# Another written order for the entry of layer 0

## The chip, the cores and the metric

The kernel runs on one core of one Trainium2 chip. The core has TensorE for matrix products (PE in the profile, its weight loads PEld), VectorE (DVE), ScalarE (ACT), GpSimd (POOL) and SyncE (SP, which here only issues loads). Products are written to PSUM, everything else lies in SBUF. The metric is the time of one execution on the device in microseconds (us), as the median of several.

## The reference

Two layers of a transformer over 512 tokens `x` and 256 context tokens `ctx`, width 1024, all in float32. Only the start of layer 0 matters here:

```python
mod = silu_c @ ada_w[l] + ada_b[l]            # for x; modc the same from c_ctx, for ctx
sh1, sc1, g1, sh2, sc2, g2 = split(mod, 6)    # parts 0 to 5
a  = rmsnorm(h, norm1_g[l]) * (1 + sc1) + sh1
ac = rmsnorm(hc, norm1_g[l]) * (1 + csc1) + csh1
u, v, q, k, vv = split(a @ w_in, ...)
kc, vvc = split(ac @ w_in[:, KV_START:], ...)
```

So before the first large product (here `q` and `k`) a small product has to give the shift and scale columns (`ada`), and each token's root mean square has to be known.

## The kernel before

Tokens lie along the free dimension, the width in eight tiles of 128 partitions (`k` = 0 to 7): `hx[k]` is 128x512 of `x`, `hc[k]` 128x256 of `ctx`. Every float32 operand of a large product is split into two fp32r parts, a rounded one by ScalarE (`copy`) and the difference by VectorE or POOL. `mm3` (lines 115 to 117) makes three products out of them, high by high, high by low, low by high. Weights `raws[k]` are split by `w_split(k)`, the difference at line 456 on POOL. All this is in the function `even`.

The order of work in the entry is written out by hand. `run` (line 48) puts each instruction behind the one that was written before it on its engine: `chain` for TensorE, `act`, `dve`, and "SP" for the loads. All these show as L49. What isn't written with them is placed by a planner, which simulates the times of the whole program.

The steps that are touched:

- `ada_step(ps, k, slab)`: one k of the product of the silu of both conditions (`cst`, 32 columns) with a slab of `ada_w`, in four column groups; TensorE. Eight of them make half a part (512 columns). `half_load(j, h)` loads the slabs of half h of part j, in two tiles of 1 MB (tag `ar`, 4 buffers). Parts: 1 scale, 0 shift.
- `half_row(ps)`: ScalarE copies the result from PSUM to `row`, TensorE turns it into columns in a bank `pt`. `half_mod(j, h, v, who)`: VectorE adds the bias and, for the scale, computes (m + 1) * gain into `self.mod`; `who` is 0 for `x`, 1 for `ctx`.
- `sums(acc, T)`: TensorE sums the squares, VectorE takes the inverse root (lines 144 to 148) and makes diagonals of it (line 185). `spread(rd)`: TensorE spreads a diagonal to a row `rx` (for `x`) or `rc` (for `ctx`) in a bank. There are three banks of tag `b`.
- `scale(k)`: VectorE multiplies `hx[k]` by the scale column and `rx`; ScalarE takes the high part. `low(k)`: VectorE takes the low one. `lagged` runs the two so that `low` is one k late. `ctx_square`, `ctx_scale`, `ctx_low`: the same for `ctx`, into `CP`.
- `project(k)`: 12 products of 512 columns into four PSUM halves `accx` (q and k for `x`). The shift is not in `scale`: `shift_cols(h)` puts the shift columns behind the ctx columns of `CP` (256 + 2), the ctx products `accc` carry them along, and they are added later as `bc`. `shifted(k)` then makes the operand with shift for the later `v0` products.
- `warm(t, n)`: n products whose result nobody reads.
- `ada_some`, `ada_ahead`: steps and loads of parts 2 to 5, which go on during the v0 products.

Of the kernel before, what the change touches and what calls it, by code (L numbers as in the profile page):

```python
# [6 lines left out]
F32 = mybir.dt.float32  # L7
# [4 lines left out]
ALU = mybir.AluOpType  # L12
AX = mybir.AxisListType.X

P = 128
D = 1024
KT = D // P
# [10 lines left out]
class Builder:  # L28
# [17 lines left out]
    def run(self, key, fn, *args, **kw):  # L46

        with self.tc.issue_after(self.tail[key].ins) if key in self.tail else ExitStack():
            self.tail[key] = fn(*args, **kw)  # L49
        return self.tail[key]  # L50
# [269 lines left out]
    def even(self):  # L320
        tc, nc, a = self.tc, self.nc, self.a
# [15 lines left out]
        for k in range(0, KT, 2):  # L337
            t = self.load(Rh, a["xT"][k * P:(k + 2) * P, :].rearrange("(k p) t -> p k t", p=P), [P, 2, TX], f"hx{k}")
# [18 lines left out]
        def half_load(j, h):  # L357

            out = []
            for k in (0, 4):  # L360
                t = self.adap.tile([P, 4, 512], F32, name=self.uid("ar"), tag="ar", bufs=4)
                c = j * D + h * 512
                src = a["ada0"][k * P:(k + 4) * P, c:c + 512].rearrange("(k p) c -> p k c", p=P)
                self.last_slab = run("SP", nc.sync.dma_start, t, src)
                out += [t[:, i, :] for i in range(4)]
            return out

        def chain(fn, *args, **kw):
            return run("PE", fn, *args, **kw) if head else fn(*args, **kw)  # L369

        def ada_step(ps, k, t):

            w = t.shape[-1] // 4
            for q in range(4):
                chain(nc.tensor.matmul, ps[32 * q:32 * q + 32, :w], cst[:, k, :], t[:, w * q:w * q + w], start=k == 0,
                      stop=k == KT - 1, skip_group_check=True)
# [18 lines left out]
        def half_row(ps):  # L395

            row = self.tmp("t")[:, :P]
            act(nc.scalar.copy, row, ps[:, :P])
            pt = self.bank()[:, :P]
            chain(nc.tensor.transpose, pt, row, self.ident)  # L400
            return row, pt.rearrange("p (q w) -> p q w", q=4)

        def half_mod(j, h, v, who):

            c = slice(j * KT + 4 * h, j * KT + 4 * h + 4)
            m = self.mod[who][:, c]
            dve(nc.vector.tensor_tensor, m, v[:, :, who], self.adab[:, c], ALU.add)
            if j:
                dve(nc.vector.scalar_tensor_tensor, m, m, 1.0, self.gain(0, 0)[:, 4 * h:4 * h + 4], ALU.add, ALU.mult)

        idle = self.wide()

        def warm(t, n):

            for _ in range(n):
                chain(nc.tensor.matmul, idle[:, :P], self.ones, t, start=True, stop=True, skip_group_check=True)
# [12 lines left out]
        def ada_some():  # L429
            if loaded:  # L430
                j, k, t = loaded.pop(0)
                if k == 0:
                    ps_of[j] = self.fill()
                ada_step(ps_of[j], k, t)
                if k == KT - 1:
                    ada_out(j, 2, ps_of.pop(j), self.bank())

        raws = []
# [11 lines left out]

        W = {}

        def w_split(k):
            t = self.adap.tile([P, 2, 512], F32R, name=self.uid("wq"), tag="wq", bufs=2) if k in (2, 5) else self.slot()
            act(nc.scalar.copy, t[:, 0, :], raws[k])
            nc.gpsimd.tensor_tensor(t[:, 1, :], raws[k], t[:, 0, :].bitcast(F32), ALU.subtract)  # L456
            W[k] = [(t[:, 0, c:c + P], t[:, 1, c:c + P]) for c in range(0, 512, P)]

        self.tail, run, head = {}, self.run, [1]
# [1 line left out]
        def act(fn, *args, **kw):  # L461
            return run("ACT", fn, *args, **kw)

        def dve(fn, *args, **kw):
            return run("DVE", fn, *args, **kw)

        sq = self.squares(hx, TX)
        slabs = {(1, 0): half_load(1, 0)}
# [15 lines left out]
        def sums(acc, T):  # L484
            rd = self.rstd_diag([(acc, T)], 1.0 / D)[0]
            self.tail["PE"], self.tail["DVE"] = self.last_sum, self.last_diag
            return rd

        def spread(rd):
            rows = self.bank()[:, :rd.shape[-1]]  # L490
            chain(nc.tensor.matmul, rows, self.ones, rd, start=True, stop=True)
            return rows

        rd = sums(sq, TX)
        ps0 = self.fill()
        for k in range(KT):
            ada_step(ps0, k, slabs[1, 0][k])
            if k == 5:
                rx = spread(rd)
            warm(slabs[1, 0][k][:, :P], 2)  # L500
        row, pt = half_row(ps0)
        warm(row, 8)
        w2 = [self.wide(), self.wide()]
        accx = [w[:, h * 512:(h + 1) * 512] for w in w2 for h in range(2)]
        keys = (0, 1, 4, 5)
# [12 lines left out]
        def shift_cols(h):  # L518
            for who in range(2):
                m = self.mod[who][:, 4 * h:4 * h + 4]  # L520
                hi, lo = [CP[:, 4 * h:4 * h + 4, i, TC + who] for i in range(2)]
                act(nc.scalar.copy, hi, m)
                dve(nc.vector.tensor_tensor, lo, m, hi.bitcast(F32), ALU.subtract)

        def shifted(k):
            for h, A, who in ((hx[k], axx[k], 0), (hc[k], axc[k], 1)):
                sh = self.modcol(0, 0, k, who)
                act(nc.scalar.activation, A[0], h, AF.Identity, bias=sh)
                dve(nc.vector.scalar_tensor_tensor, A[1], h, sh, A[0].bitcast(F32), ALU.add, ALU.subtract)
# [3 lines left out]
        def ctx_square(i):  # L533
            t = self.tmp("tq"[i % 2])[:, :TC] if i else csq
            act(nc.scalar.activation, t, hc[i], AF.Square)
            if i:
                dve(nc.vector.tensor_tensor, csq, csq, t, ALU.add)
# [8 lines left out]
        def project(k):  # L546
            for n in range(4):
                chain(self.mm3, accx[n], W[k][n], axx[k], k == 0, k == KT - 1)

        def lagged(first, second, ks):  # L550
            ks = list(ks)
            for i, k in enumerate(ks):
                first(k)
                if i:
                    second(ks[i - 1])
            second(ks[-1])

        half_mod(1, 0, pt, 0)
        w_split(0)
        w_split(1)  # L560
        lagged(scale, low, range(4))
        half_mod(1, 0, pt, 1)
        w_split(2)
# [2 lines left out]
        project(1)  # L566
        for i in range(4):
            ctx_square(i)
        ps0 = self.fill()
        for i in range(KT):  # L570
            ada_step(ps0, i, slabs[1, 1][i])
        row, pt = half_row(ps0)
        half_mod(1, 1, pt, 0)
        lagged(scale, low, range(4, 8))
        half_mod(1, 1, pt, 1)
        w_split(4)
        for i in range(4, 8):
            ctx_square(i)
        for k in (2, 3, 4):
            project(k)  # L580
        with tc.issue_after(self.tail["PE"].ins), tc.issue_after(self.tail["DVE"].ins):
            rd = sums(csq, TC)
        for k in (5, 6, 7):
            w_split(k)
        for k in (5, 6):
            project(k)
        rc = spread(rd)
        ps0 = self.fill()
        for i in range(KT):
            ada_step(ps0, i, slabs[0, 0][i])  # L590
        lagged(ctx_scale, ctx_low, range(KT))
        row, pt = half_row(ps0)
        half_mod(0, 0, pt, 0)
        half_mod(0, 0, pt, 1)
        shift_cols(0)
        project(7)
        evens = [0.125 if key < 4 else 1.0 for key in keys]
        for n in range(4):
            act(nc.scalar.mul, qk[keys[n]][:, :TX], accx[n], evens[n])
        w2 = [self.wide(), self.wide()]  # L600
        accc = [w[:, h * 512:h * 512 + TC + 2] for w in w2 for h in range(2)]
        for k in range(KT):
            if k == 3:
                ps0 = self.fill()
                for i in range(KT):
                    ada_step(ps0, i, slabs[0, 1][i])
                row, pt = half_row(ps0)
                half_mod(0, 1, pt, 0)
                half_mod(0, 1, pt, 1)
                shift_cols(1)  # L610
            for n in range(4):
                run("PE", self.mm3, accc[n], W[k][n], (CP[:, k, 0, :], CP[:, k, 1, :]), k == 0, k == KT - 1)
            if k == 4:
                head.clear()
            if k == 5:
                for i in range(4):
                    shifted(i)
            if k > 4:
                ada_some()
                ada_ahead(1)  # L620
        for n in range(4):
            t = qk[keys[n]]
# [4 lines left out]
        for n in range(4):  # L627
            t = qk[keys[n]]
# [10 lines left out]
        for k in range(KT):  # L639
            W = self.unit(a["v0"][k * P:(k + 1) * P, :], 512)  # L640
            for tb in range(6):
                c = slice(tb * P, (tb + 1) * P)
# [4 lines left out]
        for ps in acc:  # L647
            h = Rv.tile([P, 512], F32R, name=f"vhi{len(vhi)}")
# [267 lines left out]
        for k in order:  # L916
# [7 lines left out]
            if k == 4:  # L924
                low = ins
# [1108 lines left out]
```

## Time and profile before

| | |
|---|---|
| median of 3 runs | 1567.02 us (1563.9 to 1568.08) |
| profiled execution | 1566.89 us |
| its span | 1565.1 us |
| TensorE busy | 1506.8 us, 96% |
| VectorE, POOL, ScalarE busy | 1079.9, 818.3, 734.4 us |
| granted TensorE clock, mean | 0.993 |

A row of the timeline gives start and duration in us, the engine, the line, the operation, the tile written and the tiles read, the shape, and how many equal ones were merged (x). In brackets stands the idle time of the engine before it and who ended it. A merged row covers the time from the first start to the last end, so that waits in between may lie in it. A row of the stages gives the window, then busy time and count of PE, PEld, DVE, ACT and POOL, then the granted clock, the busy share of the DMA engines and GB/s. A float32 product counts as two instructions.

### The profile page before, as it was taken

How to read it: one execution, taken by the hardware profiler on the slowest of the kernel's cores; microseconds unless marked ns; L12 is line 12 of the kernel's file. 1: busy time of each engine (PE TensorE's matmuls, PEld its weight loads, DVE VectorE, ACT ScalarE, POOL GpSimd, SP SyncE). 2: the span in 40 equal slices, each digit the busy share in tenths (PEclk: the TensorE clock that was granted, in tenths of full speed). 3: DMA queues.
4: the chain of work that ended last, by engine and by line, in shares of the span. 5: the costliest groups of instructions: out<-in, count | busy, mean ns of one | idle time of the engine just before them, and what ended most of it. 6: DMA issues, size and time to landing. Idle time of an engine off the chain costs nothing.

```text
span 1565.1 us, 25189 instructions
## 1 busy us (share of the span) xinstructions
PE 1506.8 (96%) x9647; PEld 1352.6 (86%) x9647; DVE 1079.9 (69%) x1920; ACT 734.4 (47%) x1515; POOL 818.3 (52%) x558
## 2 busy tenths in 40 slices
PE   6899999999999999999999999999999999999998
PEld 4667788889999999999999988777869889999997
DVE  5532788865688788888786487665657976666665
ACT  3434567563553333333333254555556544444444
POOL 1262231051256776677776454531314399888882
PEclk9999999999999999999999999999999999999999
DMA  9583100051223333454542212110224132323201
GB/s 334 188 315 128 45 21 1 8 194 68 68 83 117 115 113 112 142 168 137 167 169 68 80 59 63 56 35 15 66 104 162 55 120 90 114 89 115 89 21 54
DMA packets 55464, 162.27 MB, mean 104 GB/s; under 512 B 6192, under 2 KB 8624, under 8 KB 47664
## 3 DMA queue, kind: packets, MB, share of 16 engines
q1 hardware_dynamic: 48288, 135.37, 25.5%
q10 hardware_dynamic: 7056, 25.30, 5.0%
q8 instruction: 75, 1.23, 0.3%
q14 instruction: 45, 0.37, 0.1%
HBM read 158.55 MB, written 2.10 MB: 103 GB/s over the span
## 4 chain that ended last, share of the span: by engine, by line
PE 81%; DVE 10%; ACT 2%; issue 2%; POOL 0%; DMA 0%; DVEq 0%; ACTq 0%; POOLq 0%
PE pw L115 11%; PE pw L116 11%; PE pw L117 11%; PE pb L116 8%; PE pb L115 8%; PE pb L117 8%; PE pf L115 4%; PE pf L116 4%; PE pf L117 4%; PE pb L1844 2%; PE pb L1833 2%; PE pw L1795 1%; PE pw L1803 1%; PE pf L369 1%; DVE t L49 1%
## 5 line engine op out<-in xcount | busy, mean ns | idle before, releaser
L115 PE MATMUL pw<-ax,w 128*128 128x384 f32 (+2 forms) x716 | 227.4, 319 | 4.5 <-DVE q L49 1.9
L992 DVE SCALAR_TENSOR_TENSOR xT<-pb,mod,xT 128x512 f32<-128x512 f32 (+3 forms) x204 | 143.2, 708 | 127.7 <-PE pb L117 127.5
L116 PE MATMUL pw<-ax,w 128*128 128x384 f32 (+2 forms) x716 | 228.0, 319 | 2.4 <-DVE ax L49 2.4
L117 PE MATMUL pw<-ax,w 128*128 128x384 f32 (+2 forms) x716 | 227.6, 318 | 0.7 <-POOL w L456 0.6
L49 POOL TENSOR_TENSOR w<-raw,w 128x512 fp32r<-128x512 f32 x122 | 185.4, 1535 | 47.3 <-ACT w L49 47.2
L92 POOL TENSOR_TENSOR w<-raw,w 128x512 fp32r<-128x512 f32 (+1 forms) x70 | 103.4, 1483 | 168.7 <-ACT w L89 153.5
L49 POOL TENSOR_TENSOR w<-t,w 128x512 fp32r<-128x512 f32 x99 | 149.2, 1510 | 55.7 <-ACT w L49 55.7
L115 PE MATMUL pb<-hh,w 128*128 128x512 f32 x480 | 171.0, 356 | 1.2 <-DVE xT L992 1.2
L117 PE MATMUL pb<-hh,w 128*128 128x512 f32 x480 | 171.5, 357 | 0.4 <-DVE w L49 0.4
L116 PE MATMUL pb<-hh,w 128*128 128x512 f32 x480 | 171.1, 356 | 0.0
L115 PE MATMUL pw<-T,w 128*128 128x384 f32 (+1 forms) x508 | 157.3, 311 | 2.5 <-DVE hs L1200 1.2
L116 PE MATMUL pw<-T,w 128*128 128x384 f32 (+1 forms) x508 | 157.7, 311 | 1.2 <-DVE T L132 1.2
L117 PE MATMUL pw<-T,w 128*128 128x384 f32 (+1 forms) x508 | 157.7, 311 | 0.0
L115 PE MATMUL pf<-ax,w 128*128 128x256 f32 (+2 forms) x460 | 150.5, 327 | 2.8 <-DVE qf L264 1.0
L117 PE MATMUL pf<-ax,w 128*128 128x256 f32 (+2 forms) x460 | 149.3, 325 | 0.0
L116 PE MATMUL pf<-ax,w 128*128 128x256 f32 (+2 forms) x460 | 148.8, 324 | 0.0
L115 PEld LDWEIGHTS pw<-ax,w 128*128 128x128 f32 x716 | 136.1, 191 | 9.5 <-DVE q L49 2.6
L116 PEld LDWEIGHTS pw<-ax,w 128*128 128x128 f32 x716 | 136.7, 191 | 7.2 <-DVE ax L49 3.2
L117 PEld LDWEIGHTS pw<-ax,w 128*128 128x128 f32 x716 | 136.6, 191 | 3.7 <-POOL w L456 1.1
L49 POOL TENSOR_TENSOR hh<-hs,hh 128x768 fp32r<-128x768 f32 (+1 forms) x42 | 77.5, 1846 | 94.9 <-ACT hh L49 68.8
L49 POOL TENSOR_TENSOR w<-rawo,w 128x512 fp32r<-128x512 f32 x59 | 103.7, 1757 | 28.7 <-ACT w L49 28.7
L240 DVE SCALAR_TENSOR_TENSOR junk<-ar,cb 128x1024 bf16<-128x1024 f32 x64 | 105.6, 1650 | 0.0
(443 smaller groups left out, 3928.0 us busy)
## 6 DMA issues: line engine op xcount, KB each, us to landing
raw<-ffn_in SPq DMA_DIRECT2D x44, 1024.0 KB, 5.4
ar<-ada SPq DMA_DIRECT2D x24, 1024.0 KB, 7.3
ar<-ada ACTq DMA_DIRECT2D x48, 512.0 KB, 3.6
rawo<-ffn_out SPq DMA_DIRECT2D x88, 256.0 KB, 3.0
raw<-odd_out SPq DMA_DIRECT2D x28, 256.0 KB, 2.6
raw<-qk SPq DMA_DIRECT2D x16, 256.0 KB, 6.1
raw<-uv SPq DMA_DIRECT2D x16, 256.0 KB, 3.1
raw<-even_out SPq DMA_DIRECT2D x8, 512.0 KB, 3.5
```

Of the source, the lines that this page charges most:

```text
L49: self.tail[key] = fn(*args, **kw)
L92: eng.tensor_tensor(lo, raw, hi.bitcast(F32), ALU.subtract)
L115: mm(out, s[0], m[0], start=start, stop=False, **kw)
L116: mm(out, s[0], m[1], start=False, stop=False, **kw)
L117: return mm(out, s[1], m[0], start=False, stop=stop, **kw)
L240: return self.nc.vector.scalar_tensor_tensor(junk, t, 1.0, self.cb[who], ALU.mult, ALU.mult, accum_out=self.acc[who][:, col:col + 1])
L369: return run("PE", fn, *args, **kw) if head else fn(*args, **kw)
L992: ins = self.nc.vector.scalar_tensor_tensor(h, ps[:, r], self.modcol(l, j, m, who), h, ALU.mult, ALU.add)
L1795: nc.tensor.matmul(ps[:, st:en], Q, K[g][p][:, b0 * P:b1 * P], start=p == 0, stop=p == 1, skip_group_check=True)
L1803: last = nc.tensor.matmul(ps[:, en:en + TC], Q, K[g][p][:, TX:], start=p == 0 and not edge, stop=p == 1, skip_group_check=True)
L1833: last = nc.tensor.transpose(pt[:, x * P:(x + 1) * P], es[2 * (x % 2) + x // 2][:, kb * P:(kb + 1) * P], self.ident)
L1844: nc.tensor.matmul(po[64 * h:64 * h + 64, :], V[vb][:, 64 * g:64 * g + 64], t[:, h * TC:h * TC + TC], start=kb == 0, stop=kb == nb - 1, sk ...
```

## The change

The first steps run without warming products between them, the row factors are spread after all eight steps, and six warming products stand behind the turn of the row. The first two weights are split by VectorE instead of POOL. `half_row` is divided into the copy and the turn (`half_turn`), and other TensorE work is written between the two. For the scale, `half_mod` writes the sum of column and bias back into PSUM and reads it from there. The ctx chain (`ctx_scale`, `ctx_low`) comes after the shift columns of half 0 instead of before them, and its squares, the sums and the splits of weights 5 to 7 stand elsewhere. The steps of (0,0) come ahead of `project(5)`, those of (0,1) ahead of the ctx products, and `shifted(0..3)` after the first ctx group. SP's order is not touched.

```diff
+        def half_turn(row):
             pt = self.bank()[:, :P]
             chain(nc.tensor.transpose, pt, row, self.ident)
...
-            dve(nc.vector.tensor_tensor, m, v[:, :, who], self.adab[:, c], ALU.add)
+            dve(nc.vector.tensor_tensor, v[:, :, who] if j else m, v[:, :, who], self.adab[:, c], ALU.add)
             if j:
-                dve(nc.vector.scalar_tensor_tensor, m, m, 1.0, self.gain(0, 0)[:, 4 * h:4 * h + 4], ALU.add, ALU.mult)
+                dve(nc.vector.scalar_tensor_tensor, m, v[:, :, who], 1.0, self.gain(0, 0)[:, 4 * h:4 * h + 4], ALU.add,
+                    ALU.mult)
...
         rd = sums(sq, TX)
+        w_split(0, nc.vector)
+        w_split(1, nc.vector)
         ps0 = self.fill()
         for k in range(KT):
             ada_step(ps0, k, slabs[1, 0][k])
-            if k == 5:
-                rx = spread(rd)
-            warm(slabs[1, 0][k][:, :P], 2)
-        row, pt = half_row(ps0)
-        warm(row, 8)
+        row = half_row(ps0)
+        rx = spread(rd)
+        pt = half_turn(row)
+        warm(slabs[1, 0][0][:, :P], 6)
...
+        def half_steps(j, h):
+            ps = self.fill()
+            for i in range(KT):
+                ada_step(ps, i, slabs[j, h][i])
+            return half_row(ps)
...
         half_mod(1, 0, pt, 0)
-        w_split(0)
-        w_split(1)
         lagged(scale, low, range(4))
...
         for i in range(4):
             ctx_square(i)
-        ps0 = self.fill()
-        for i in range(KT):
-            ada_step(ps0, i, slabs[1, 1][i])
-        row, pt = half_row(ps0)
-        half_mod(1, 1, pt, 0)
-        lagged(scale, low, range(4, 8))
-        half_mod(1, 1, pt, 1)
-        w_split(4)
+        row = half_steps(1, 1)
         for i in range(4, 8):
             ctx_square(i)
-        for k in (2, 3, 4):
-            project(k)
+        w_split(4)
+        project(2)
+        pt = half_turn(row)
+        half_mod(1, 1, pt, 0)
+        lagged(scale, low, range(4, 8), (5, 6, 7))
+        half_mod(1, 1, pt, 1)
+        project(3)
         with tc.issue_after(self.tail["PE"].ins), tc.issue_after(self.tail["DVE"].ins):
             rd = sums(csq, TC)
-        for k in (5, 6, 7):
-            w_split(k)
-        for k in (5, 6):
-            project(k)
+        project(4)
+        row = half_steps(0, 0)
+        project(5)
         rc = spread(rd)
-        ps0 = self.fill()
-        for i in range(KT):
-            ada_step(ps0, i, slabs[0, 0][i])
+        pt = half_turn(row)
+        for who in range(2):
+            half_mod(0, 0, pt, who)
+        shift_cols(0)
         lagged(ctx_scale, ctx_low, range(KT))
-        row, pt = half_row(ps0)
-        half_mod(0, 0, pt, 0)
-        half_mod(0, 0, pt, 1)
-        shift_cols(0)
+        project(6)
         project(7)
         evens = [0.125 if key < 4 else 1.0 for key in keys]
         for n in range(4):
             act(nc.scalar.mul, qk[keys[n]][:, :TX], accx[n], evens[n])
+        row = half_steps(0, 1)
...
         for k in range(KT):
-            if k == 3:
-                ps0 = self.fill()
-                for i in range(KT):
-                    ada_step(ps0, i, slabs[0, 1][i])
-                row, pt = half_row(ps0)
-                half_mod(0, 1, pt, 0)
-                half_mod(0, 1, pt, 1)
-                shift_cols(1)
             for n in range(4):
                 run("PE", self.mm3, accc[n], W[k][n], (CP[:, k, 0, :], CP[:, k, 1, :]), k == 0, k == KT - 1)
+            if k == 0:
+                pt = half_turn(row)
+                for who in range(2):
+                    half_mod(0, 1, pt, who)
+                shift_cols(1)
+                for i in range(4):
+                    shifted(i)
...
-            if k == 5:
-                for i in range(4):
-                    shifted(i)
```

`w_split(k, eng)` takes the difference on `eng` in `dve`'s order if one is given, and `lagged(first, second, ks, also)` calls `w_split(k)` behind the k that stand in `also`.

More of the change, by code (lines that the diff above doesn't have):

```diff
@@ L398, in half_row @@
             act(nc.scalar.copy, row, ps[:, :P])
+            return row
+        def half_turn(row):
             pt = self.bank()[:, :P]
             chain(nc.tensor.transpose, pt, row, self.ident)
-            return row, pt.rearrange("p (q w) -> p q w", q=4)
+            return pt.rearrange("p (q w) -> p q w", q=4)
         def half_mod(j, h, v, who):
@@ L451, in even, with w_split @@
         W = {}
-        def w_split(k):
+        def w_split(k, eng=None):
             t = self.adap.tile([P, 2, 512], F32R, name=self.uid("wq"), tag="wq", bufs=2) if k in (2, 5) else self.slot()
             act(nc.scalar.copy, t[:, 0, :], raws[k])
-            nc.gpsimd.tensor_tensor(t[:, 1, :], raws[k], t[:, 0, :].bitcast(F32), ALU.subtract)
+            low = t[:, 1, :], raws[k], t[:, 0, :].bitcast(F32), ALU.subtract
+            if eng:
+                dve(eng.tensor_tensor, *low)
+            else:
+                nc.gpsimd.tensor_tensor(*low)
             W[k] = [(t[:, 0, c:c + P], t[:, 1, c:c + P]) for c in range(0, 512, P)]
@@ L548, in project, with lagged @@
                 chain(self.mm3, accx[n], W[k][n], axx[k], k == 0, k == KT - 1)
-        def lagged(first, second, ks):
-            ks = list(ks)
+        def lagged(first, second, ks, also=()):
             for i, k in enumerate(ks):
@@ L555, in lagged @@
                     second(ks[i - 1])
+                if k in also:
+                    w_split(k)
             second(ks[-1])
+        def half_steps(j, h):
[3 more added lines that the diff above has]
+            return half_row(ps)
         half_mod(1, 0, pt, 0)
-        w_split(0)
-        w_split(1)
         lagged(scale, low, range(4))
```

## The prediction

> **What bounds the kernel now.** I read the page first, then the stages (busy time by window, with the granted clock), then the timeline of TensorE, VectorE and ScalarE over the first 82 us, then the landings of the loads.
>
> ```profile
> span 1565.1 us, 25189 instructions
> PE 1506.8 (96%) x9647; PEld 1352.6 (86%) x9647; DVE 1079.9 (69%) x1920; ACT 734.4 (47%) x1515; POOL 818.3 (52%) x558
> ...
> PE 81%; DVE 10%; ACT 2%; issue 2%; POOL 0%; DMA 0%; DVEq 0%; ACTq 0%; POOLq 0%
> ```
>
> TensorE is busy for 96% of the span and is 81% of the chain that ended last. So a microsecond in which TensorE idles, runs slowly or does needless products in the entry should be a microsecond of the whole, unless a later stage waits for something else. The next rows (start, duration; then engine, line, out<-in) are the first chain, up to the first projection.
>
> ```profile
> 14.02 0.66 PE L49 MATMUL pf<-ar,cst 128*32 128x128 f32 x8
> ...
> 16.29 0.87 DVE L185 TENSOR_SCALAR q<-ident,sm 128x128 f32<-128x128 f32 x4
> ...
> 17.17 0.43 PE L49 MATMUL pf<-ar,cst 128*32 128x128 f32 x8
> ...
> 20.52 1.13 PE L49 MATMUL pb<-q,ones 128*128 128x512 f32 x2
> ...
> 23.01 0.42 PE L49 MATMUL pf<-ar,cst 128*32 128x128 f32 x8
> ...
> 23.51 0.27 ACT L49 COPY t<-pf 128x128 f32<-128x128 f32 x1 [12.97 <-PE pf L49]
> ...
> 23.92 0.27 PE L49 MATMUL pb<-ident,t 128*128 128x128 f32 x1
> ...
> 24.37 2.50 POOL L456 TENSOR_TENSOR w<-raw,w 128x512 fp32r<-128x512 f32 x2 [23.17 <-ACT w L49]
> 24.42 1.24 DVE L49 SCALAR_TENSOR_TENSOR mod<-mod,gains 128x4 f32<-128x4 f32 x1
> ...
> 25.70 1.41 DVE L49 SCALAR_TENSOR_TENSOR hx<-hx,mod,pb 128x512 f32<-128x512 f32 x2
> ...
> 27.13 0.69 DVE L49 TENSOR_TENSOR ax<-hx,ax 128x512 fp32r<-128x512 f32 x1
> 27.15 0.51 PE L115 MATMUL pw<-ax,w 128*128 128x512 f32 x1 [1.17 <-ACT ax L49]
> ```
>
> The eight ada steps take from 14.02 to 23.43, because warming products stand between them. The diagonal of the row factors is ready at 17.16, yet its spread runs at 20.52. The `mod` step with two SBUF inputs takes 1.24 us beside POOL's split. The middle of the entry follows.
>
> ```profile
> 33.31 1.96 PE L49 MATMUL pf<-ar,cst 128*32 128x128 f32 x64
> ...
> 35.79 0.48 PE L115 MATMUL pw<-ax,wq 128*128 128x512 f32 x1
> ...
> 36.27 0.16 DVE L49 SCALAR_TENSOR_TENSOR mod<-mod,gains 128x4 f32<-128x4 f32 x1
> ...
> 36.47 1.41 DVE L49 SCALAR_TENSOR_TENSOR hx<-hx,mod,pb 128x512 f32<-128x512 f32 x2
> ...
> 41.81 0.15 DVE L49 TENSOR_TENSOR mod<-pb,adab 128x4 f32<-128x4 f32 x1
> ...
> 46.83 0.71 PE L165 MATMUL pb<-ones,sq 128*128 128x128 f32 x4 [1.15 <-DVE sq L49]
> 47.30 0.47 PE L115 MATMUL pw<-ax,wq 128*128 128x512 f32 x1
> ...
> ...
> 49.74 0.48 DVE L185 TENSOR_SCALAR q<-ident,sm 128x128 f32<-128x128 f32 x2
> ...
> 52.88 0.60 PE L49 MATMUL pb<-q,ones 128*128 128x256 f32 x2
> 53.41 1.96 PE L49 MATMUL pf<-ar,cst 128*32 128x128 f32 x64
> ...
> 53.52 0.88 DVE L49 SCALAR_TENSOR_TENSOR hc<-hc,mod,pb 128x256 f32<-128x256 f32 x2 [3.30 <-PE pb L49]
> ...
> 59.59 0.48 PE L49 MATMUL pb<-ident,t 128*128 128x128 f32 x1 [4.22 <-ACT t L49]
> 59.72 0.78 PE L115 MATMUL pw<-ax,w 128*128 128x512 f32 x1
> ...
> 60.10 0.23 DVE L49 TENSOR_TENSOR mod<-pb,adab 128x4 f32<-128x4 f32 x2 [0.28 <-PE pb L49]
> ...
> 62.66 1.08 ACT L49 ACTIVATE f<-pw 128x512 f32<-128x512 f32 x2 [2.07 <-PE pw L117]
> ...
> 64.78 0.28 PE L115 MATMUL pw<-cp,w 128*128 128x258 f32 x1
> ...
> 75.90 0.39 PE L115 MATMUL pw<-cp,w 128*128 128x258 f32 x1
> ...
> 81.76 0.39 PE L115 MATMUL pb<-w,ax 128*128 128x512 f32 x1
> ```
>
> TensorE stands for 4.22 us at 55.37, because the copy of the ada row is queued on ScalarE behind eight ctx casts. The stages show what that costs besides:
>
> ```profile
> 56.00:58.00 2.00, 0.00 (x0) 0.00 (x0) 2.00 (x7) 1.22 (x3) 0.00 (x0) 0.93 0.79 311
> 58.00:64.50 6.50, 4.92 (x12) 3.91 (x13) 2.18 (x9) 2.35 (x7) 0.00 (x0) 0.50 0.50 210
> 82.00:120.00 38.00, 38.00 (x194) 23.61 (x193) 13.93 (x26) 10.42 (x21) 21.20 (x16) 1.00 0.83 302
> ```
>
> The third figure from the end is the clock: half speed up to 64.5, so project(7) takes 64.78-59.72 = 5.06 us. At full speed two projections take 52.88-47.30 = 5.58, 2.79 each. From 82 on TensorE is full.
>
> **The change part by part.** Nearly all of the entry is chained in written order on each engine, so I walk the new order with these durations. "Entry end" is the start of the v0 products, 81.76 before.
>
> *Warming dropped, spread moved, splits 0 and 1 to VectorE.* TensorE starts the steps at 14.02 as before. Eight steps cost 1.96 at full speed. In before a step's eight instructions fall from 0.66 to 0.43 by 17.17, so I count half speed up to 17.2, twice 0.245 or 0.49 a step (6.5 steps), then 0.245: end about 17.55. Spread 1.13 and transposition 0.27 on top: about 18.95. (Bounds of the end: 16.0 all fast, 17.9 all at half speed, and the spread up to 1 later.) ScalarE's row copy, 0.27, lies under the spread. VectorE meanwhile does two split differences after 17.16. No row has this operation on VectorE: nearest is 0.69 for the same shape (27.13), with POOL active twice that at most by the 1.24 row; I take 0.69, since POOL does nothing before 24.37, so VectorE is free at 18.6. They need the raw tiles, which land by 7.9+9.3 = 17.2 at the latest:
>
> ```profile
> L49 SPq DMA_DIRECT2D raw<-qk x2: 340/340/340, 6.5 to 7.9; - x2
> ...
> DMA to landing us min/median/max: 8.6/9.0/9.3
> ```
>
> *`mod` through PSUM.* Bounds 0.16 (36.27) and 1.24 (24.42); I take 0.16, because the long row has two SBUF inputs beside POOL and the new form reads PSUM and finds POOL idle. With its sum 0.4 in all: first scale at about 19.45 instead of 25.70. The six left warming products run beside this. First projection 6.25 us earlier: 20.9. The same distance as before (33.31-27.15 = 6.16) puts the steps of (1,1) at 27.1 to 29.05.
>
> *Row of (1,1) turned after project(2); splits 5 to 7 between the scales.* project(2) to 31.85, turn to 32.1; the wait for the copy goes, since project(2) covers it. VectorE's chain of scales and lows (41.81-36.47 = 5.34) runs 32.5 to 37.9. POOL's splits fall into it now: zero to about 1.5 more, from the 1.24 against 0.16, I take 0.5. The rows of the ctx squares (to 29 plus) come out in time. TensorE: project(3) to 34.7, sums 0.47 (46.83 to 47.30), project(4) to 38.0. In before 35.79 to 47.30 holds three projections (8.37) and those sums: 2.67 of waits for scales, splits and squares, which now have project(2) and (3) ahead of them.
>
> *Steps of (0,0) ahead of project(5), ctx chain after the shift columns.* Steps to 39.95, project(5) to 42.75. The rsqrt chain behind the sums (47.54 to 50.22, 2.68), which VectorE starts once it is through `mod` at 38.8, ends at 41.5, so the spread (0.53, 52.88 to 53.41) and the turn end near 43.6. VectorE: `mod` and shift columns about 0.7 (three pairs of 0.23, 60.10), then the ctx chain (53.52 to 59.82, which is 60.10 less its idle 0.28; 6.3) from 44.4 to 50.7, while TensorE runs project(6), project(7) to 49.2 and the steps of (0,1) to 51.1. So the 4.22 and the 2.27 of half speed (5.06-2.79) go.
>
> *Late next: the evacuation of the projections.* On ScalarE it is queued behind the ctx casts: 50.8, 51.9 for two, 53.0 for four (1.08 a pair, 62.66). The ctx products wait for those banks: 0.8 at 51.1 and 0.35 between the pairs. Bounds: 0 to 3 (the 6.3 chain fully uncovered by another 2 us).
>
> *Steps and turn of (0,1), shifted(0..3).* The copy comes behind the evacuation at about 53.2, the turn behind ctx product group 0 (1.465 a group: (81.76-75.90)/4): 54.0. Seven groups, 10.25, and two n=2 ada steps between them, about 1.9: entry end 66.2. The `shifted` pairs lie on ScalarE and VectorE beside the groups.
>
> *Queues.*
>
> ```profile
> L49 SPq DMA_DIRECT2D ar<-ada x4: 379/379/379, 20.5 to 35.3; - x4
> ...
> DMA to landing us min/median/max: 6.0/9.1/10.8
> ```
>
> SP's order is unchanged; its raw tiles 5 to 7 and the slabs (0,0) and (0,1) are asked for when earlier tiles come free, and those all come earlier. In before the slowest of the four slabs took 10.8 and the last was asked for at 35.3, so (0,1) had landed by 46.1 at the latest, and 49.2 is when it is needed now. Both tiles of (0,0) can be asked for from about 20.5, by which the steps of (1,0) are over: landed by about 32, needed at 38.0.
>
> The first slab is held by the six warming products until about 20.2, against the 20.5 at which SP moved on before: nothing lost. POOL loses two splits (2.50) and has nothing else there.
>
> *Sum.* 81.76-66.2 = 15.6: 6.25 at the front, 2.67 of waits, 6.5 of stall and half clock, about 1.3 of small waits (turns, evacuation in before), less 1.15 of new wait. I take off 1.6 for a dozen new handoffs at 0.1 to 0.15 (23.43 to 23.51 into the row copy and 23.78 to 23.92 out of it are two such): 14. The profiled execution took 1566.89 with span 1565.1, and the median shown is 1567.02, so it stands for the runs. 1566.9-14 = 1553.
>
> **Rivals.**
>
> *A bank wait and a clock drop.* Sums of ctx need a third bank `b`. If buffers are given out in turn, theirs is that of `rx`, held until scale(7): VectorE's 32.5 plus four scales and two lows of 0.7, 36.7, up to 38 with POOL, while TensorE is there at 34.7: 2 to 3.3 idle. In before the clock fell after 2.35 us of idleness (a mean of 0.93 over 56 to 58 is half speed for 0.28, so from 57.72; idle since 53.41+1.96 = 55.37) and cost 2.27. Together about 5: 1558. Against it: any free bank does, and two of three are then free if they are picked so.
> [...]
>
> *The clock stays low.* If narrow steps don't count as work, the clock is still half when projections begin, and the first of them run at half speed for up to one stretch as at 59.7 (4.8 us, losing about 2.4), with steps and spread 1.5 later: gain 10, 1557. Against: clock 1.00 in the stage from 82 with steps in it.
>
> *The loads take it back.* The v0 stage moves 302 GB/s at 0.83 DMA share. If the slabs of parts 2 to 5 arrive no earlier, TensorE waits and the end stays: 1566. Against: the first of them are asked for when the steps of (0,0) free their tiles, and these end at 39.95 instead of 55.37; and TensorE, not DMA, is full there.
>
> *Slower.* One mechanism in the same stage: TensorE waits for a slab longer than the 2.35 us of above and goes on at half speed, 2.35+2.27 = 4.6 each. Ada steps stand behind each of v0's eight k, so there is room for it. From the fifth wait on it costs over 14+4.7 = 19 and the kernel is slower; with five it is 1566.9-14+23 = 1576. Against: DMA would have to lose its spare 0.17, and 1.00 is the clock over 82 to 120.
>
> **How the numbers follow.** Forecast (10 to 18 gained, 1549 to 1557): 0.63. Bank wait 0.11, low clock 0.08, loads take it back 0.12, slower 0.06. The first three are faster, 0.82. A gain of 18 is the sum without handoffs (15.6), without the new wait (1.15), and with steps all fast (1.55, 16.0 for 17.55); 10 is the forecast less a spread 1 later, POOL's other 1 and an evacuation wait of 3 for 1.15. The top, 1561, lies above both smaller gains and leaves the last two out (0.18). 0.3% is 4.7 us, about what a measurement of this kernel can tell from no change.
>
> **What would show it.** First scale near 19.5, `mod` step 0.16, first projection near 21; no TensorE wait over 1.5 us before the v0 products; clock 1.00 from 18 to 70; ctx products waiting about 1 us for ScalarE's evacuation; v0 products starting at 66 to 69. Wrong if v0 starts there and the page's span is still within 5 us of 1565, if the sums of ctx wait on VectorE's scale(7), or if steps wait on `ar` landings.

## The result and the profile after

The changed kernel takes 1552.24 us (median of 4 runs, 1550.48 to 1552.66) against 1565.83 for the kernel before beside it: ratio 0.9911, 95% interval 0.9893 to 0.9928, so 13.6 us less (by the interval 11.3 to 16.8). A second comparison (below) gave 0.9896 (0.9881 to 0.9911). The forecast was 1553.

The page of the changed kernel:

```profile
span 1550.1 us, 25119 instructions
PE 1496.6 (97%) x9611; PEld 1344.5 (87%) x9611; DVE 1080.4 (70%) x1922; ACT 736.4 (48%) x1515; POOL 816.4 (53%) x556
```

The span is 15.0 shorter. TensorE's busy time fell by only 10.2; the rest is idle time that went. Its timeline through the entry, with the rows that answer to those of before:

```profile
13.93 3.64 PE L49 MATMUL pf<-ar,cst 128*32 128x128 f32 x64
...
20.70 0.50 PE L115 MATMUL pw<-ax,w 128*128 128x512 f32 x1 [0.55 <-ACT ax L49]
...
26.88 1.95 PE L49 MATMUL pf<-ar,cst 128*32 128x128 f32 x64
...
34.53 0.61 PE L165 MATMUL pb<-ones,sq 128*128 128x128 f32 x4
...
38.16 1.95 PE L49 MATMUL pf<-ar,cst 128*32 128x128 f32 x64
...
43.55 0.70 PE L49 MATMUL pb<-q,ones 128*128 128x256 f32 x2 [0.46 <-DVE q L185]
...
49.77 1.96 PE L49 MATMUL pf<-ar,cst 128*32 128x128 f32 x64
51.87 0.39 PE L115 MATMUL pw<-cp,w 128*128 128x258 f32 x1
...
66.20 0.50 PE L115 MATMUL pb<-w,ax 128*128 128x512 f32 x1
```

The eight steps are over at 17.57 instead of 23.43; the first projection is at 20.70, not 27.15. The stall of 4.22 is gone, and so is the half clock behind it, as the stage shows (clock third from the end):

```profile
18.00:60.00 42.00, 40.57 (x376) 33.21 (x375) 32.48 (x78) 23.28 (x53) 10.21 (x8) 1.00 0.93 342
```

The first v0 product starts at 66.20 instead of 81.76: 15.56 us. To see what becomes of that, here are pieces of the chain that ended last, with their starts, before and then after:

```profile
127.47 3.62 PE pf L369 x32
400.57 1.12 PE pb L170 x10
971.60 2.60 DMA raw<-q
1555.60 1.34 PE pf L170 x12
```

```profile
112.03 3.62 PE pf L369 x32
382.86 1.12 PE pb L170 x10
954.97 2.56 DMA raw<-q
1540.59 1.34 PE pf L170 x12
```

The lead is 15.44 at the end of the v0 stage, then 17.71, 16.63 and 15.01. Nothing in the v0 stage takes any of it back. What changes later changes in both directions, and part of it can be seen: before ran at half speed around 320, after did not there (1.00 over 302 to 309), but did around 1240, where before did not (1.00 over 1253 to 1261). The stages, before first and then after:

```profile
317.00:324.00 7.00, 5.97 (x20) 5.29 (x21) 3.61 (x12) 2.83 (x4) 0.00 (x0) 0.51 0.43 139
```

```profile
1237.00:1245.00 8.00, 6.10 (x31) 5.25 (x30) 7.77 (x10) 3.63 (x7) 7.67 (x7) 0.79 0.43 133
```

Two more such stretches, of 3.4 us each, lie between these points and cancel: after ran at half speed around 968 (0.66 over 966 to 971), and across it the lead fell from 16.67 to 15.07; before did so around 1216 (0.66 over 1214 to 1219), and across it the lead rose from 15.03 to 16.53. A third, in before around 971 (0.57 over 969 to 973), left the lead as it was; the chain there runs through a load (971.60).

The last step, from 15.0 in the profiles to 13.6 in the medians, is that before's profiled run (1566.89) lies 1.06 above its median there, and after's (1551.89) 0.35 below.

### The profile page after: what moved, and what is told of

It is laid out like the page before. It is cut to its first block, busy times and chain, and to the rows that moved or that the text cites. A ratio compares the mean times of both kernels' runs of the same rounds, so it can differ in the third digit from the quotient of the medians.

```text
span 1550.1 us, 25119 instructions
## 1 busy us (share of the span) xinstructions
PE 1496.6 (97%) x9611; PEld 1344.5 (87%) x9611; DVE 1080.4 (70%) x1922; ACT 736.4 (48%) x1515; POOL 816.4 (53%) x556
## 4 chain that ended last, share of the span: by engine, by line
PE 82%; DVE 13%; ACT 3%; issue 2%; DMA 0%; POOL 0%; DVEq 0%; SPq 0%; ACTq 0%; POOLq 0%
PE pw L116 11%; PE pw L115 11%; PE pw L117 11%; PE pb L115 8%; PE pb L116 8%; PE pb L117 8%; PE pf L115 4%; PE pf L116 4%; PE pf L117 4%; PE pb L1851 2%; PE pb L1840 2%; PE pw L1802 1%; PE pw L1810 1%; PE pf L369 1%; DVE t L49 1%
```

## The experiments

"Entry end" is the start of the first v0 product in the profile of each kernel. The first four ask whether the front and the middle of the change each carry through.

**The front alone** (the kernel before, with this; its `half_mod` also goes through PSUM, as in the change):

```diff
+        w_split(0, nc.vector)
+        w_split(1, nc.vector)
         ps0 = self.fill()
         for k in range(KT):
             ada_step(ps0, k, slabs[1, 0][k])
-            if k == 5:
-                rx = spread(rd)
-            warm(slabs[1, 0][k][:, :P], 2)
-        row, pt = half_row(ps0)
-        warm(row, 8)
+        row = half_row(ps0)
+        rx = spread(rd)
+        pt = half_turn(row)
+        warm(slabs[1, 0][0][:, :P], 6)
...
         half_mod(1, 0, pt, 0)
-        w_split(0)
-        w_split(1)
```

> The kernel before with the front of the change alone: steps without warming between them, spread and turn behind them, weights 0 and 1 split on VectorE, mod through PSUM; all behind it in the old order. Theory (what TensorE saves at the front is carried through to the end): first projection near 20.7 us instead of 27.15, entry end (first v0 product) near 75.4 instead of 81.76, time 6 to 6.5 us under before. Rival (the old order waits behind it for splits, ctx squares and loads anyway): first projection near 20.7 too, but entry end 78.5 or later, time at most 3 us under before.

```profile
52.68 0.33 PE L49 MATMUL pb<-ident,t 128*128 128x128 f32 x1 [4.22 <-ACT t L49]
...
74.17 0.39 PE L115 MATMUL pb<-w,ax 128*128 128x512 f32 x1
...
53.00:57.00 4.00, 4.00 (x13) 3.10 (x12) 0.50 (x4) 1.38 (x4) 0.00 (x0) 0.57 0.31 131
```

The old stall comes 6.9 us earlier (59.59 to 52.68), and the entry ends 7.6 earlier, since half speed lasts only 0.43*4/0.5 = 3.4 us here (48 to 53 and 57 to 60 stand at 1.00). Ratio 0.9966 (0.9953 to 0.9978), about 5.3 us; the interval is 3.4 to 7.4, so it holds the 6 to 6.5 expected and not the 3 of the rival. The front is not swallowed by what waits behind it.

**The middle alone** (the changed kernel with the four front edits reversed):

> The changed kernel with the old front (warming between the steps, spread behind step 5, splits 0 and 1 on POOL behind the first mod step, mod through SBUF). Theory (parts add): first projection at 27.15, from there the same 45.5 us as in the changed kernel (20.70 to 66.20), entry end near 72.6, time 9 us under before. Rival (the front is swallowed and the order behind it does nearly all): entry end near 67 to 69, time 12 us or more under before.

Entry end 72.17, 9.6 earlier than before; ratio 0.9954 (0.9935 to 0.9972), about 7 us where 9 were expected, which the interval (4.4 to 10.2) still holds. With the front alone that is 7.6 + 9.6 = 17.2 at the entry against 15.56 for both; of the 1.6 too much 0.7 is the shorter half clock in the front's profile, which the middle removes anyway, and 0.8 is chance ahead of the first projection, which came at 20.29 with the front alone (20.70 in the changed kernel) and at 26.80 with the middle alone (27.15 before). By time it is 12.5 for the two ratios added, against 13.6 and 15.8 between the medians for the change. The parts add, within what these intervals can tell.

**The old place of the row of (0,0)** (the changed kernel):

```diff
-        row = half_steps(0, 0)
+        ps0 = self.fill()
+        for i in range(KT):
+            ada_step(ps0, i, slabs[0, 0][i])
         project(5)
         rc = spread(rd)
+        lagged(ctx_scale, ctx_low, range(KT))
+        row = half_row(ps0)
         pt = half_turn(row)
         for who in range(2):
             half_mod(0, 0, pt, who)
         shift_cols(0)
-        lagged(ctx_scale, ctx_low, range(KT))
         project(6)
```

> The changed kernel with one old place put back: the row of (0,0) is copied, turned and used behind the ctx casts, ahead of project(6). Theory: TensorE idles about 6 us from 44 to 50, the clock falls, project(6) and (7) run partly at half speed and lose about 2.4; entry end near 74.5, time 8 us over the changed kernel. Rival (VectorE's chain of 6.3 us sets the end of the entry, not TensorE, so TensorE's idle time mostly costs nothing): entry end up to 70, 2 to 4 us over.

```profile
50.49 0.47 PE L49 MATMUL pb<-ident,t 128*128 128x128 f32 x1 [6.10 <-ACT t L49]
50.61 0.77 PE L115 MATMUL pw<-ax,w 128*128 128x512 f32 x1
...
58.63 1.95 PE L49 MATMUL pf<-ar,cst 128*32 128x128 f32 x64
...
74.58 0.50 PE L115 MATMUL pb<-w,ax 128*128 128x512 f32 x1
...
50.00:58.00 8.00, 7.51 (x23) 6.01 (x24) 1.08 (x6) 1.36 (x6) 0.00 (x0) 0.65 0.00 0
```

Entry end 8.4 later than in the changed kernel, and ratio 0.9960 (0.9944 to 0.9976) to before, so about 7.7 us of the change (0.9960 against 0.9911, from two comparisons) are lost by this order alone. Here TensorE's idle time costs its full length, and the clock more on top: 6.10 and the 2.4 measured next make 8.5, about the 8.4 seen.

**The same stall filled with products nobody reads** (the kernel just shown, with this):

```diff
         rc = spread(rd)
+        fb = self.bank()[:, :P]
+        for _ in range(25):
+            chain(nc.tensor.matmul, fb, self.ones, self.ones, start=True, stop=True, skip_group_check=True)
         lagged(ctx_scale, ctx_low, range(KT))
```

> The same as the one before, with 25 products that nobody reads (about 5.3 us) on TensorE in the idle time. Theory (the half clock is a price by itself): clock 1.00, the idle time is as long but filled, project(6) and (7) take 2.8 each, entry end 2 to 2.5 us before that of the unfilled stall, near 72. Rival (the clock costs nothing, only the wait does): entry end within 0.5 us of the unfilled one.

```profile
43.74 5.74 PE L49 MATMUL pb<-ones 128*128 128x128 f32 x50
...
50.09 0.48 PE L115 MATMUL pw<-ax,w 128*128 128x512 f32 x1
...
55.75 1.95 PE L49 MATMUL pf<-ar,cst 128*32 128x128 f32 x64
...
71.69 0.50 PE L115 MATMUL pb<-w,ax 128*128 128x512 f32 x1
...
50.00:58.00 8.00, 7.99 (x92) 6.54 (x93) 0.74 (x5) 2.69 (x7) 0.00 (x0) 1.00 0.08 12
```

Project(6) and (7) take 50.09 to 55.75 here and 50.61 to 58.63 in the unfilled one: 5.66 against 8.02, at a clock of 1.00 and 0.65 over 50 to 58. So here the half clock is worth 2.4 us by itself. The entry ends 2.9 earlier, but 0.5 of that stands at the first projection already (20.39 for 20.89). The times (0.9950, 0.9933 to 0.9966) lie on the same side, but their intervals overlap. By the trace, warming products thus have a use where a stall can't be removed; the times don't show it.

The next four take the front apart. They were run once each, so their profiles are read and not their times. A profile has some chance in the front: the same first steps took 3.64 us in the first profile of the changed kernel and 2.52 in the second (below), where the steps of (1,1) took 1.95, and the first projection came at 20.70 and 20.30. From the first projection to the entry end it was 45.50 and 45.51. So a difference of 0.4 at the entry end means nothing by itself, and this distance tells more.

**Without the last six warming products:**

> The changed kernel without its last six warming products. Theory (they fill 1.9 us ahead of the first projection, too short an idle time for the clock to fall): first projection at 20.7, clock 1.00 from 18 to 60, entry end within 0.3 us of 66.2. Rival (they hold the clock up): half speed from about 20 on for 3.4 us, entry end 1.5 us or more later.

```profile
20.17 0.50 PE L115 MATMUL pw<-ax,w 128*128 128x512 f32 x1 [1.89 <-ACT ax L49]
...
65.63 0.50 PE L115 MATMUL pb<-w,ax 128*128 128x512 f32 x1
...
18.00:60.00 42.00, 39.23 (x368) 32.22 (x367) 33.41 (x78) 23.47 (x53) 10.80 (x8) 1.00 0.92 341
```

TensorE idles 1.89 us and the clock stays. The entry ends 0.57 earlier, outside the 0.3 expected, but that lies ahead of the first projection (the steps took 2.72); from there on it is 45.46. In this profile the six products do nothing.

**Splits 0 and 1 on POOL behind the first mod step again**, with mod through PSUM, and then with mod through SBUF:

```diff
-        w_split(0, nc.vector)
-        w_split(1, nc.vector)
...
         half_mod(1, 0, pt, 0)
+        w_split(0)
+        w_split(1)
```

> The changed kernel with the differences of weights 0 and 1 on POOL and behind the first mod step, as in before; mod still through PSUM. Theory (what made the old mod step 1.24 us long is two SBUF inputs beside POOL, so the PSUM form is untouched): mod step 0.16 us although POOL runs, first scale at 19.2, entry end within 0.4 us of 66.2. Rival (POOL slows any small VectorE step): mod step about 1.2, first scale 20.3, entry end 67.2.

> The same, and mod through SBUF as in before. Theory: mod step about 1.2 us again beside POOL's split, first scale 20.3, entry end near 67.2. Rival (the old long step had another cause, such as the first use of a tile): 0.16, entry end 66.2.

The PSUM form first, the SBUF form behind it:

```profile
17.95 2.51 POOL L465 TENSOR_TENSOR w<-raw,w 128x512 fp32r<-128x512 f32 x2 [16.75 <-ACT w L49]
...
18.77 0.16 DVE L49 SCALAR_TENSOR_TENSOR mod<-pb,gains 128x4 f32<-128x4 f32 x1
...
30.88 0.42 DVE L49 TENSOR_TENSOR sq<-sq,q 128x256 f32<-128x256 f32 x1
```

```profile
18.19 2.50 POOL L465 TENSOR_TENSOR w<-raw,w 128x512 fp32r<-128x512 f32 x2 [16.99 <-ACT w L49]
...
18.65 0.83 DVE L49 SCALAR_TENSOR_TENSOR mod<-mod,gains 128x4 f32<-128x4 f32 x1
```

With PSUM the step takes 0.16 in the middle of POOL's work; with SBUF it takes 0.83 and ends at 19.48, when POOL's first split, half of the merged 2.50, ends (19.44). In before's trace it ended at 25.66 and POOL's first split at 25.62. The other three `mod` steps of the SBUF form took 1.12, 0.60 and 1.06 and each ended 0.02 after a split of POOL. Lengths that differ and ends that agree: in these five steps that looks like a wait for the running POOL instruction to end, not like a slower step.

Entry ends: 65.03 with PSUM and 66.33 with SBUF, so mod through PSUM is worth about 1.3 us, of which the two `mod` steps on the path (0.83 and 0.60 for 0.16 each) make 1.1. Neither entry end was as expected (66.2 within 0.4, and 67.2). The first tells most: with the splits back on POOL the entry ended 1.2 us earlier than in the changed kernel. Of this 0.3 stands at the first projection (20.42 for 20.70), no more than the two profiles of the changed kernel differ by. The other 0.9 is the last ctx square: 0.42 and 0.43 with the late splits, 1.34 in both profiles of the changed kernel. So the move of the splits to VectorE gained nothing here, and the square came out 0.9 worse with it. My 0.16 was right, but for a case that didn't need the move.

**Two warming products behind each step again:**

> The changed kernel with two warming products behind each of the first eight steps again (16 in all), the rest of the change kept. Theory (the dropped products are nearly the whole gain of the front): the steps take 14 to 23.4, spread and turn behind them, first projection near 26.8, entry end near 72.3. Rival (the early spread or the splits are the gain): first projection before 23, entry end under 69.

```profile
26.64 0.49 PE L115 MATMUL pw<-ax,w 128*128 128x512 f32 x1 [0.55 <-ACT ax L49]
...
72.11 0.50 PE L115 MATMUL pb<-w,ax 128*128 128x512 f32 x1
```

Of the front's gain nearly all, 72.11-66.20 = 5.9 us (6.3 against the second profile of the changed kernel), is the dropped warming.

**Warming ahead of the sums**, `warm(self.ones, 32)` while TensorE waits for `x`:

> The changed kernel with 32 warming products on a tile of ones ahead of the first sums, while TensorE waits for x. Theory (the sums and the first steps run at half speed, 2.05 and 3.64 us, and the front waits for them): sums about 1.1, steps end near 16.2 behind the landing of the slabs, first scale near 18.2 instead of 19.24, entry end near 65.2. Rival (the loads and the split of the raw weights end last there): first scale within 0.3 us of 19.24.

```profile
11.86 1.16 PE L165 MATMUL pb<-ones,sq 128*128 128x128 f32 x8 [1.78 <-DVE sq L205]
...
15.10 1.08 PE L49 MATMUL pf<-ar,cst 128*32 128x128 f32 x32 [1.07 <-DMA ar<-ada]
```

The sums take 1.16 instead of 2.05, and the steps run as two halves of 1.08, where all eight took 3.64; now the second half waits 1.07 for a slab. That the front ran slower without this warming stands in the durations alone: the changed kernel's clock reads 1.00 over 12 to 18 too. Entry end 65.30, 0.9 earlier than in the first profile of the changed kernel and 0.5 than in the second; time 0.9902 (0.9870 to 0.9934), not to be told from the change. Its profiled run took 1547.87, but its median is 1551.62, so that number alone says nothing.

**The kernel before, once more:**

> The kernel before once more, for a second profile. [...]

```profile
60.05 0.47 PE L49 MATMUL pb<-ident,t 128*128 128x128 f32 x1 [4.22 <-ACT t L49]
...
82.47 0.39 PE L115 MATMUL pb<-w,ax 128*128 128x512 f32 x1
...
58.00:66.00 8.00, 5.95 (x17) 4.81 (x18) 2.64 (x10) 3.05 (x9) 0.00 (x0) 0.57 0.45 192
```

Again 4.22 idle, and 0.43*8/0.5 = 6.9 us at half speed; entry end 0.7 later, at 82.47; 0.4 of it stands at the first projection already (27.57 for 27.15). The same idle time with 3.4 us of half speed stands in the front alone, so the length isn't fixed, but these two profiles of before don't show it to vary.

**Early warming, late POOL splits, and weight 4 split on VectorE together; and the changed kernel again beside it:**

> The changed kernel with 32 warming products ahead of the first sums, weights 0 and 1 split on POOL behind the first mod step, and weight 4 split on VectorE. Theory (the sums at half speed, and the last square waiting for POOL's split of weight 4, still cost about 1 us each): first projection near 19.5 us, the last ctx square 0.42 long, the mod step of (1,1) near 31 instead of 32.84, entry end near 64.0, time 2 us under the changed kernel. Rival (the landing of the raw tiles 4 to 6 and the slabs ends last there): mod step of (1,1) earlier, but entry end 65.5 or later.

> The changed kernel once more, beside the one before it here. [...] Rival (its first profile was a lucky draw): entry end 67.5 or later, and under 11 us gained.

Combined first, the change behind it:

```profile
30.16 0.42 DVE L49 TENSOR_TENSOR sq<-sq,q 128x256 f32<-128x256 f32 x1
...
35.58 3.07 DVE L49 TENSOR_TENSOR ax<-hx,ax 128x512 fp32r<-128x512 f32 x2
...
64.81 0.50 PE L115 MATMUL pb<-w,ax 128*128 128x512 f32 x1
```

```profile
13.96 2.52 PE L49 MATMUL pf<-ar,cst 128*32 128x128 f32 x64
...
31.20 1.34 DVE L49 TENSOR_TENSOR sq<-sq,q 128x256 f32<-128x256 f32 x1 [0.52 <-ACT w L49]
...
65.81 0.50 PE L115 MATMUL pb<-w,ax 128*128 128x512 f32 x1
```

The last square is short again (0.42 for 1.34), with no split of POOL beside it, but two lows beside POOL's splits now take 3.07, where two took 1.46 at 22.09. So the entry ends 1.0 earlier than beside it, between what the theory (64.0) and the rival (65.5) gave, and all of it stands at the first projection already (19.33 for 20.30): behind it the freed square and the later lows cancel. Times: 1550.18, ratio 0.9889 (0.9871 to 0.9907), against 1551.67, 0.9896 (0.9881 to 0.9911): the combined version is the lowest median here, but not distinguishable from the change. The change itself gained 15.8 between the medians, and its entry end came 0.39 earlier than in its first profile: neither the 67.5 nor the under 11 of the rival. Its mean granted clock is 0.996, for 0.997 in the first profile, which met two stretches of half speed behind the entry (around 968 and 1241). The piece of twelve instructions at 302 of its chain took 2.93 us, for 1.60 in the first profile, where the clock reads 1.00 over 302 to 309.

## Why the prediction was right

The walk along the engines held. By its own steps, forecast and then measured: first scale 19.45 and 19.24; first projection 20.9 and 20.70; steps of (1,1) 27.1 and 26.88; sums 34.7 (project(3)'s end) and 34.53; steps of (0,0) 38.0 and 38.16; steps of (0,1) 49.2 and 49.77; ctx products 51.9 and 51.87; entry end 66.2 and 66.20. That it agrees this closely is partly luck: the first steps were to end at 17.55 and did at 17.57 in this profile, but at 16.48 in the second, and the entry ended at 65.81 there.

Two terms inside it were mis-sized and offset each other.

```profile
31.57 1.34 DVE L49 TENSOR_TENSOR sq<-sq,q 128x256 f32<-128x256 f32 x1 [0.52 <-ACT w L49]
...
33.23 1.41 DVE L49 SCALAR_TENSOR_TENSOR hx<-hx,mod,pb 128x512 f32<-128x512 f32 x2
...
35.94 1.80 DVE L49 TENSOR_TENSOR ax<-hx,ax 128x512 fp32r<-128x512 f32 x1
...
39.97 0.16 DVE L49 TENSOR_TENSOR pb<-pb,adab 128x4 f32<-128x4 f32 x1
```

VectorE's chain of scales and lows took 39.97-33.23 = 6.74, not 5.84: POOL's splits cost 1.4, near the upper bound of 1.5, where I took 0.5. It also began 0.7 late, because the last square took 1.34 instead of 0.42 beside POOL's split (31.35 to 32.64), which I hadn't seen. That gave TensorE a wait of 0.46 for the diagonal, forecast as none. In exchange the new wait for ScalarE's evacuation, 1.15 in the forecast, was about 0.3: 0.14 ahead of the first ctx product (51.73 to 51.87), and 0.15 ahead of the next pair of banks (52.58 to 52.85, where 0.12 lies between other products). TensorE came later, and the evacuation did not.

The 1.6 taken off for handoffs isn't to be found in the entry, where the full 15.6 came. The median gain of 13.6 doesn't show them either: its interval, 11.3 to 16.8, holds 15.6 as well as 14, and in the second comparison it was 15.8 (1567.47 to 1551.67). So 14 was right in size, but no run shows that allowance, and that 14 came nearer to 13.6 than 15.6 did is luck. What sets off each of the later half-speed stretches was not followed up.

The rivals: the sums of ctx did not wait for scale(7) (they ran at 34.53, scale(7) at 37.66), so no bank was waited for. The clock did not stay low (1.00 from 18 to 60). The loads took nothing back, 15.44 of 15.56 being left behind the v0 stage. No wait with half speed came in v0 (clock 1.00 over 66 to 115, TensorE busy for all of it).

## What to carry to other kernels

Before counting on warming products, ask what they delay: here they cost about 6 us ahead of the first projection, full speed came without them (the steps of (1,1) took 1.95, the clock was 1.00 from 18 to 60), and where a stall remained they were worth 2.4 by the trace. When an engine's own small copy or turn is queued behind a long chain on another engine, write independent products between the copy and its use. On an engine-by-engine walk, look for every VectorE instruction with two SBUF inputs beside a POOL instruction, not only for the one that the change is about: here the `mod` step took 0.60 to 1.24 us instead of 0.16, the last ctx square 1.34 instead of 0.42. And compare two profiles from a common point behind what varies by chance, here the first projection, before a difference of half a microsecond is read as an effect.

## What the runs showed of the hardware

An idle time of 4.22 us on TensorE brought half speed each time, of 3.4 us (front alone) or 6.9 us (before, 0.57 over 57 to 65, and before again); 1.89 us brought none, in one profile (1.00 over 18 to 60). The start varied too: in before the clock fell 2.35 us into the idle time (55.37 to 57.72), and in the front alone not before 53 (1.00 over 48 to 53), when TensorE had already been at work again since 52.68. What decides over start and length these runs don't show. And whether VectorE or POOL comes first by 0.2 us decided over 0.9: the last ctx square took 0.42 when it started at 30.88, ahead of POOL's split at 31.06, and 1.34 when it started at 31.57, behind the one at 31.35.
